# Where matmul operands begin in a partition: one start modulo 512 bytes for all of them

## The chip, the cores and the metric

One core of a Trainium2 chip runs the whole program: two blocks of a small language model over 256 tokens of width 1024. The metric is the device time of one execution in microseconds (us), the median of several runs.

## What is computed

The first block is a gated MLP mixer and a windowed attention; the second is a retention layer, an MLA attention and, behind each of these two, a PEER layer with 128 x 128 experts. Nearly all the work is projections of 256 tokens; of the two PEER layers, this is the core:

```python
q = (xb @ w_q).reshape(T, 8, 2, 128)
s = jnp.einsum('thcd,hckd->thck', q, sub_keys)          # scores of the sub-keys
# top 16 of each half, top 16 of their sums -> eidx, gate = softmax(top_s)
h = jax.nn.gelu(jnp.einsum('thkd,td->thk', u[eidx], xb))
return jnp.einsum('thk,thkd->td', gate * h, v[eidx])
```

The kernel computes it densely: `gelu(X u^T)` for all 16384 experts, times a table of gates that is zero outside the chosen ones, times `v`.

## The kernel before, in words

Activations lie transposed in SBUF: `xh` and `xl` are 128 partitions x 8 x 256 tokens. Every fp32 factor is held as two fp32r halves, a high and a low one. `mm3` (L146 to L150) multiplies two such pairs with three matmuls into one accumulator: high x high (L148), then L149, then L150.

- `unit` (L102) loads a block of 128 x 1024 weights over SP's DMA queue into a buffer `w` and splits it, 512 columns at a time, into `wh` (a cast on ScalarE, ACT, L139) and `wl` (a subtraction on VectorE, DVE, L140). Buffers are taken in turn from the pools that are open: `weights` has 3 `w` and 5 pairs `wh`/`wl` all the time; `w2` adds 3 and 5 in the first block and retention, each PEER layer adds 2 pairs, MLA 2 and 5.
- `o2` (L238): a slice of 128 weight columns is the stationary operand, 256 columns of `xh` or `xl` (in attention `xg`, in MLA the latents `cqT`, `ckT`) are the moving one: 24 matmuls a unit, 7872 on `xh`/`xl` in all. In PEER these are the `u` blocks.
- `out_unit` (L243): the stationary operand is a slice of 128 tokens of the activation (`wdh`/`wdl` in PEER, `yh`/`yl`, `oh`/`ol`), 512 columns of `wh`/`wl` move: 12 matmuls a unit. In PEER these are the `v` blocks.
- `o1_unit` (L229): the same with `xh`/`xl` as the stationary operand.

A tile scheduler sets order and waits from the code's order and priorities. A PEER layer runs thus: 16 `u` blocks with the query units between them; 48 `u` blocks, with the search for the best experts (`route`, DVE) woven in; 64 `u` blocks, with the gates of half the experts woven in (first pass: `gates`, L1143 and on, DVE and ACT, and small fp16 matmuls, L1169); 62 `v` blocks with the other half's gates (second pass); the 66 `v` blocks left.

Tiles stand in a partition one behind the other, in the order in which pools are opened and tiles asked for, each rounded up to 32 bytes. So small tiles push what stands behind them off any round address. The starts modulo 512 bytes, read from the built program:

| operand | before |
|---|---|
| `xh`, `xl` | 128 |
| `w`, `wh`, `wl` of `weights` | 160 |
| the same of every pool added later | 288 |
| `wdh`, `wdl`; MLA's `oh`, `ol` | 288 |
| `yh`, `yl` of the MLP mixer / of retention; `y0`, `y1` of attention | 32 / 96; 416 |
| `xg0`, `xg1` | 352 |
| `cqT`, `ckT` (two tiles each) | 288 |

A slice of a weight tile for `o2` begins a multiple of 512 bytes further, a 256-column slice of `xh` a multiple of 1024: they keep their tile's start modulo 512. Which buffer a matmul reads follows from the program's order.

Of the kernel before, what the change touches and what calls it, by code (L numbers as in the profile page):

```python
# [10 lines left out]
F32 = mybir.dt.float32  # L11
F32R = mybir.dt.float32r
# [9 lines left out]
KB = 8  # L22
# [10 lines left out]
U2 = 64  # L33
PASSES = ((0, 64, 64, 6), (64, 64, 62, 6))
NT = 8
GSCALE = 2.0 ** 15


class Net:
    def __init__(s, ctx, tc, aps):  # L40
        s.ctx, s.tc, s.nc, s.d = ctx, tc, tc.nc, aps
        nc = s.nc
        s.cp = ctx.enter_context(tc.tile_pool(name="consts", bufs=1))

        s.wbufs, s.pbufs, s.taken = [], [], [0, 0]
        s.more_weights(ctx, "weights", 3, NSPLIT)
        tc.cur_priority += 4 * AHEAD
        s.sp = ctx.enter_context(tc.tile_pool(name="small", bufs=4))
        s.ps = ctx.enter_context(tc.tile_pool(name="psum", bufs=4, space=bass.MemoryType.PSUM))
        s.xh = s.cp.tile([128, KB, 256], F32R, name="xh")  # L50
        s.xl = s.cp.tile([128, KB, 256], F32R, name="xl")
        s.iota = s.cp.tile([128, 128], F32, name="iota")
        nc.gpsimd.iota(s.iota, pattern=[[1, 128]], base=0, channel_multiplier=0,
                       allow_small_or_imprecise_dtypes=True)
        s.ident = s.cp.tile([128, 128], F32, name="ident")
        nc.gpsimd.memset(s.ident, 1.0)
        nc.gpsimd.affine_select(s.ident, s.ident, pattern=[[1, 128]], compare_op=ALU.is_equal, fill=0.0,
                                base=0, channel_multiplier=-1)
        s.eps = s.cp.tile([128, 1], F32, name="eps")
        nc.vector.memset(s.eps, EPS)  # L60
        with s.urgent():
            s.warm(s.eps)
        s.ident_r = s.cp.tile([128, 128], F32R, name="ident_r")
        nc.vector.tensor_copy(s.ident_r, s.ident)
# [81 lines left out]
    def mm3(s, out, a, b, start, stop):  # L146
# [2 lines left out]
        s.nc.tensor.matmul(out, a[0], b[1], start=False, stop=False)  # L149
        s.nc.tensor.matmul(out, a[1], b[0], start=False, stop=stop)  # L150

    def bcast(s, pool, ap, n, name, **kw):
        t = pool.tile([128, n], F32, name=name, **kw)
        s.nc.sync.dma_start(t, bass.AP(tensor=ap.tensor, offset=ap.offset, ap=[[0, 128], [1, n]]))
        return t

    def transposes(s, src, n):
# [160 lines left out]
    def gmlp(s, first, begin):  # L318
        nc, d = s.nc, s.d
        s.first = first  # L320
        s.h = first.tile([128, 2, D], F32, name="h")
        s.gains = first.tile([128, 2, KB], F32, name="gains")
        with ExitStack() as es:
            p = es.enter_context(s.tc.tile_pool(name="pa", bufs=1))
            with s.urgent():
# [18 lines left out]
            nc.sync.dma_start(s.gains, d["b_gains"].rearrange("p (a k) -> p a k", a=2))  # L344
            X = (s.xh, s.xl)
            v = p.tile([128, 2, 2048], F32, name="v")
            st = p.tile([128, 2, 4, 6], F32, name="vst")
            for c in range(4):
                outs = [s.mm(), s.mm()] if c else begun
                if c:  # L350
# [4 lines left out]
            lg = s.bcast(p, d["a_ln_g"], 2048, "lg")  # L355
# [83 lines left out]
    def swa(s, begun, begin):  # L439
        nc, d = s.nc, s.d  # L440
        with ExitStack() as es:
            p = es.enter_context(s.tc.tile_pool(name="pb", bufs=1))
# [3 lines left out]
            m = s.first.tile([128, D], F32, name="trash", tag="trash", bufs=1)[:, :384]  # L446
# [9 lines left out]
            kv = p.tile([128, 2, 256], F32, name="kv")  # L456
            kd = p.tile([128, 2, 2, 2, 64], F32, name="kd")
            sg = p.tile([128, 8, 256], F32, name="sg")
            xg = [p.tile([128, KB, 256], F32R, name=f"xg{i}") for i in range(2)]

            def gain_x():
                nc.vector.tensor_tensor(sg, s.xh.bitcast(F32), s.xl.bitcast(F32), op=ALU.add)
# [4 lines left out]
            fg = s.bcast(p, d["final_norm_g"], D, "fg")  # L467
            bkv = s.bcast(p, d["b_kv"], 256, "bkv")
            bq = s.bcast(p, d["b_bq"], D, "bq")
            sink = s.bcast(p, d["b_sinks"], 16, "sink")  # L470
            cs = p.tile([128, 2, 2, 32], F32, name="cs")
            nc.sync.dma_start(cs, d["swa_cs"].rearrange("p (a t f) -> p a t f", a=2, t=2))

# [179 lines left out]
    def retention(s, begun, begin):  # L653
        nc, d = s.nc, s.d
        with ExitStack() as es:
            p = es.enter_context(s.tc.tile_pool(name="pc", bufs=1))

            l = s.bcast(p, d["decay"], 8, "l")
            y, w, m, q0 = (p.tile([128, 8], F32, name=f"lg{i}") for i in range(4))
            nc.scalar.activation(y, l, AF.Exp)  # L660
            nc.vector.tensor_scalar(w, y, -1.0, 1.0, op0=ALU.mult, op1=ALU.add)
            nc.scalar.activation(q0, w, AF.Ln)
# [3 lines left out]
            nc.vector.reciprocal(w, w)  # L666
            nc.vector.tensor_tensor(q0, q0, w, op=ALU.mult)
            nc.vector.tensor_tensor(q0, q0, m, op=ALU.subtract)
            lgam = p.tile([128, 8], F32, name="lgam")
            nc.vector.scalar_tensor_tensor(lgam, q0, -1.0, y, op0=ALU.mult, op1=ALU.mult)  # L670
            nc.vector.tensor_scalar(m, m, -2.0, None, op0=ALU.mult)
            nc.vector.tensor_tensor(m, m, y, op=ALU.mult)
# [60 lines left out]
            def v_side(h):  # L733
                return [lambda f=f, tt=tt: f(h, tt) for f in (v_out, mix) for tt in range(2)]
# [3 lines left out]
            for c in range(8):  # L738
                tag = "acc" if c % 2 else "mm"
                outs[c] = [s.mm(tag), s.mm(tag)] if c else begun  # L740
                ap, c0 = (d["r_qk"], c * 4) if c < 4 else (d["r_v"], c * 4 - 16)
# [3 lines left out]
                s.weave([lambda u=u: s.o1_unit(s.unit(ap[c0 + u]), u, KB, X, outs[c]) for u in range(4)],  # L745
                        more[:2] + side[c - 1] + more[2:])
            late = v_side(3)
            gng = p.tile([128, 16], F32, name="gng")
            gnb = p.tile([128, 16], F32, name="gnb")
            nc.sync.dma_start(gng, d["gn_g"])  # L750
            nc.sync.dma_start(gnb, d["gn_b"])
            for t in (gng, gnb):
# [44 lines left out]
    def mla(s, begun, begin):  # L797
        nc, d = s.nc, s.d
        with ExitStack() as es:
            s.more_weights(es, "we", 2, NSPLIT)  # L800
            p = es.enter_context(s.tc.tile_pool(name="pe", bufs=1))
# [8 lines left out]
            cq = p.tile([128, 2, 384], F32, name="cq")  # L810
            ck = p.tile([128, 2, 256], F32, name="ck")
            kr = p.tile([128, 2, 2, 64], F32, name="kr")
            cqT = [p.tile([128, 3, 256], F32R, name=f"cqT{i}") for i in range(2)]
            ckT = [p.tile([128, 2, 256], F32R, name=f"ckT{i}") for i in range(2)]

            def latent(tt):
                for c, gain, a in ((cq, qg, acc[tt][0][:, :384]), (ck, kg, acc[tt][1][:, :256])):
# [11 lines left out]
            w = s.unit(d["m_uqr"][:, :1024]), s.unit(d["m_uqr"][:, 1024:])  # L829
# [28 lines left out]
            for u in range(2):  # L858
                w = s.unit(d["m_ukn"][u])
# [142 lines left out]
    def gate_tables(s, p, scratch, tabs):  # L1002
# [26 lines left out]
        rest = scratch[:, 0, :256]  # L1029
        nc.vector.tensor_scalar(rest, tp[:, :256], GSCALE, None, op0=ALU.mult)  # L1030
        nc.vector.tensor_copy(tabs[2][:, 0], rest)
# [15 lines left out]
    def peer(s, i, outs, begin):  # L1047
        nc, d = s.nc, s.d
        with ExitStack() as es:
# [53 lines left out]
            def gate(t0, b0, nb, act):  # L1103
                gp = s.gates(pg, t0, b0, nb, tabs, t0 // NT * act % 8 < act)
                hv = hst[:, b0:b0 + nb, t0:t0 + NT].rearrange("p b t -> p t b")
                nc.vector.scalar_tensor_tensor(hv, gp[:, :NT * nb].rearrange("p (t b) -> p t b", b=nb),  # L1106
                                               1.0 / (GSCALE * ALPHA), hv,
                                               op0=ALU.mult, op1=ALU.mult)
# [17 lines left out]
            for b0, nb, n, act in PASSES:  # L1126
                s.weave(blocks[:n], [lambda t=t: gate(t, b0, nb, act) for t in range(0, 256, NT)])
                blocks = blocks[n:]
# [14 lines left out]
    def gates(s, p, t0, b0, nb, tabs, act):  # L1143

        nc = s.nc
        i1t, i2t, gt = tabs
        sl = slice(t0, t0 + NT)
        a = p.tile([128, NT, 128], F16, name="ga", tag="ga", bufs=2)
        if act:
# [120 lines left out]
```

## Time and profile before

| | |
|---|---|
| median of 3 runs | 2291.69 us (2288.92 to 2292.26) |
| the profiled execution | 2291.83 us, its span 2290.1 us |
| TensorE (PE) busy | 2254.2 us, 98% |
| VectorE (DVE) busy | 1878.2 us, 82% |
| ScalarE (ACT) busy | 1532.3 us, 67% |
| granted clock of TensorE, mean | 0.997 |

The span is the time from the first to the last instruction; 1.7 us of the execution lie outside it. Ends of matmuls are modelled, since one begins before the last has drained: a matmul's row of 0.28 us does not mean 0.28 us of the engine. What it costs is the distance between two starts. PEld is the load of a stationary operand, which runs beside the matmul before.

### The profile page before, as it was taken

The numbers are of one execution on the slowest core, as the hardware profiler recorded it, in microseconds if no ns is written. First come the engines' busy times: TensorE is split into PE (matmuls) and PEld (weight loads), VectorE is DVE, ScalarE is ACT, GpSimd is POOL, SyncE is SP. The second block draws the span as 40 slices with busy tenths as digits, with TensorE's granted clock in tenths as the row PEclk, the third lists the DMA queues.
The fourth block names the chain that finished last, engine by engine and source line by source line (L and its number), as shares of the span: only waits on it lengthen the run. The fifth ranks groups of instructions, "written<-read, shape, count | busy, mean of one in ns | idle before, by whom it ended". The sixth has DMA issues, their size and how long they took to land. (4 is left out here: it accounts for less than half of the span.)

```text
span 2290.1 us, 43064 instructions
## 1 busy us (share of the span) xinstructions
PE 2254.2 (98%) x15726; PEld 2004.5 (88%) x15726; DVE 1878.2 (82%) x3685; ACT 1532.3 (67%) x3404; POOL 6.7 (0%) x15
## 2 busy tenths in 40 slices
PE   8999999999999999999999999999999999999998
PEld 6998877898999999977788878899999998777887
DVE  6867877567899899999986666689989999999666
ACT  5545865565555788888865546555569888887554
POOL 0000000000000000000000000000000000000000
PEclk9999999999999999999999999999999999999999
DMA  8655354354555555545455654355565554545564
GB/s 300 198 175 181 118 164 158 128 177 134 173 174 178 191 171 171 167 157 165 164 188 192 206 176 140 120 169 171 178 194 167 170 171 158 166 162 185 188 211 139
DMA packets 109224, 394.55 MB, mean 172 GB/s; under 512 B 12882, under 2 KB 13522, under 8 KB 108243
## 3 DMA queue, kind: packets, MB, share of 16 engines
q1 hardware_dynamic: 109010, 391.80, 52.4%
q8 instruction: 123, 2.02, 0.3%
q14 instruction: 91, 0.74, 0.1%
HBM read 390.70 MB, written 1.05 MB: 171 GB/s over the span
## 5 line engine op out<-in xcount | busy, mean ns | idle before, releaser
L139 ACT CAST wh<-w 128x512 fp32r<-128x512 f32 x1427 | 870.0, 614 | 556.6 <-PE mm L149 202.3
L140 DVE TENSOR_TENSOR wl<-w,wh 128x512 fp32r<-128x512 f32 x1427 | 970.7, 688 | 295.2 <-ACT wh L139 275.4
L148 PE MATMUL mm<-xh,wh 128*128 128x256 f32 x2624 | 745.9, 284 | 0.0
L149 PE MATMUL mm<-xl,wh 128*128 128x256 f32 x2624 | 739.0, 282 | 0.0
L150 PE MATMUL mm<-xh,wl 128*128 128x256 f32 x2624 | 738.2, 281 | 0.0
L148 PEld LDWEIGHTS mm<-xh,wh 128*128 128x128 f32 x2624 | 495.2, 189 | 1.7 <-issue 0.2
L149 PEld LDWEIGHTS mm<-xl,wh 128*128 128x128 f32 x2624 | 493.9, 188 | 1.7 <-issue 0.5
L150 PEld LDWEIGHTS mm<-xh,wl 128*128 128x128 f32 x2624 | 494.4, 188 | 0.4 <-DVE wl L140 0.4
L150 PE MATMUL acc<-wh,wdl 128*128 128x512 f32 x1024 | 404.2, 395 | 5.4 <-DVE wdl L140 5.2
L148 PE MATMUL acc<-wh,wdh 128*128 128x512 f32 x1024 | 408.5, 399 | 0.0
L149 PE MATMUL acc<-wl,wdh 128*128 128x512 f32 x1024 | 402.8, 393 | 0.0
L1155 ACT ACTIVATE gq<-iota,tab 128x128 bf16<-128x128 f32 x768 | 267.8, 394 | 5.6 <-DVE tab L1027 2.1
L150 PEld LDWEIGHTS acc<-wh,wdl 128*128 128x128 f32 x1024 | 192.3, 188 | 53.6 <-DVE wdl L140 8.9
L149 PEld LDWEIGHTS acc<-wl,wdh 128*128 128x128 f32 x1024 | 192.7, 188 | 42.2
L148 PEld LDWEIGHTS acc<-wh,wdh 128*128 128x128 f32 x1024 | 192.6, 188 | 41.0
L1106 DVE SCALAR_TENSOR_TENSOR hst<-mm,hst 128x512 f32<-128x512 f32 x128 | 172.7, 1349 | 0.0
L1164 DVE TENSOR_TENSOR gb<-ge,tabg 128x1024 f16<-128x1024 f16 x128 | 157.4, 1230 | 0.0
L139 ACT CAST wdh<-hst 128x256 fp32r<-128x256 f32 x256 | 102.7, 403 | 77.6 <-PE acc L149 69.2
L140 DVE TENSOR_TENSOR wdl<-hst,wdh 128x256 fp32r<-128x256 f32 x256 | 110.8, 433 | 31.0 <-ACT wdh L139 30.3
L1156 ACT ACTIVATE ga<-gq 128x512 f16<-128x512 bf16 x192 | 120.4, 627 | 2.7
L148 PE MATMUL mm<-wh,xh 128*128 128x512 f32 (+1 forms) x272 | 110.6, 406 | 0.3 <-ACT xh L139 0.2
L150 PE MATMUL mm<-wh,xl 128*128 128x512 f32 (+1 forms) x272 | 106.9, 394 | 0.5 <-DVE xl L140 0.3
(343 smaller groups left out, 2305.0 us busy)
## 6 DMA issues: line engine op xcount, KB each, us to landing
w<-in_p_u SPq DMA_DIRECT2D x256, 512.0 KB, 3.6
w<-in_p_v SPq DMA_DIRECT2D x256, 512.0 KB, 3.7
w<-in_p_q SPq DMA_DIRECT2D x32, 512.0 KB, 3.5
w<-in_a_v SPq DMA_DIRECT2D x16, 512.0 KB, 5.7
w<-in_a_g SPq DMA_DIRECT2D x16, 512.0 KB, 3.5
w<-in_a_u SPq DMA_DIRECT2D x16, 512.0 KB, 3.6
w<-in_a_out SPq DMA_DIRECT2D x16, 512.0 KB, 3.5
w<-in_r_qk SPq DMA_DIRECT2D x16, 512.0 KB, 3.5
```

Of the source, the lines that this page charges most:

```text
L139: s.nc.scalar.copy(hi, src)
L140: s.nc.vector.tensor_tensor(lo, src, hi.bitcast(F32), op=ALU.subtract)
L148: s.nc.tensor.matmul(out, a[0], b[0], start=start, stop=False)
L149: s.nc.tensor.matmul(out, a[0], b[1], start=False, stop=False)
L150: s.nc.tensor.matmul(out, a[1], b[0], start=False, stop=stop)
L1106: nc.vector.scalar_tensor_tensor(hv, gp[:, :NT * nb].rearrange("p (t b) -> p t b", b=nb), 1.0 / (GSCALE * ALPHA), hv, op0=ALU.mult, op1=AL ...
L1155: nc.scalar.activation(q[:, j, :], s.iota, AF.Square, scale=-1.0, bias=i2t[:, t:t + 1])
L1156: nc.scalar.activation(a[:, j0:j0 + 4, :], q, AF.Relu, scale=-1.0, bias=1.0)
L1164: nc.vector.tensor_tensor(b, e[:, None].to_broadcast([128, 2, NT, nb]), gt[:, :, sl, None].to_broadcast([128, 2, NT, nb]), op=ALU.mult)
```

## The change

No instruction is added, removed or moved: engine by engine the built programs have the same instructions in the same order with the same waits. What differs is where tiles stand. `xh` and `xl` get a pool of their own at the front, behind a pad of 56 words; small tiles (`sink`, `l`, `lgam`, `gng`, `gnb`, `vst`, `gains`) are put into rooms of whole 512 bytes; `apart` sets 48 words (192 bytes) ahead of `xg` and of the latents and fills up to 512 behind. Afterwards every fp32r operand of a matmul, moving or stationary, begins at 160 modulo 512, but for `xh`/`xl`, `xg`, `cqT` and `ckT`, which begin at 352 (160 + 192).

```diff
+LINE = 512
+EPS_ROOM = 48
+X_PAD = 56
+APART = 48
...
+        front = ctx.enter_context(tc.tile_pool(name="front", bufs=1))
+        front.tile([128, X_PAD], F32, name="pad")
+        s.xh = front.tile([128, KB, 256], F32R, name="xh")
+        s.xl = front.tile([128, KB, 256], F32R, name="xl")
+        s.sp = ctx.enter_context(tc.tile_pool(name="small", bufs=4))
         s.cp = ctx.enter_context(tc.tile_pool(name="consts", bufs=1))
+        s.eps = s.cp.tile([128, EPS_ROOM], F32, name="eps")[:, 0:1]
...
-        s.sp = ctx.enter_context(tc.tile_pool(name="small", bufs=4))
         s.ps = ctx.enter_context(tc.tile_pool(name="psum", bufs=4, space=bass.MemoryType.PSUM))
-        s.xh = s.cp.tile([128, KB, 256], F32R, name="xh")
-        s.xl = s.cp.tile([128, KB, 256], F32R, name="xl")
...
+    def lined(pool, n, name):
+        per = LINE // 4
+        return pool.tile([128, -(-n // per) * per], F32, name=name)[:, :n]
...
+    def apart(pool, shapes):
+        pool.tile([128, APART], F32, name="gap")
+        tiles = [pool.tile(shape, F32R, name=name) for shape, name in shapes]
+        return tiles, pool.tile([128, LINE // 4 - APART], F32, name="behind")
...
-        s.gains = first.tile([128, 2, KB], F32, name="gains")
+        s.gains = s.lined(first, 2 * KB, "gains").rearrange("p (a k) -> p a k", a=2)
...
-            xg = [p.tile([128, KB, 256], F32R, name=f"xg{i}") for i in range(2)]
+            xg, small = s.apart(p, [([128, KB, 256], f"xg{i}") for i in range(2)])
...
-            sink = s.bcast(p, d["b_sinks"], 16, "sink")
+            sink = small[:, :16]
+            s.spread(sink, d["b_sinks"])
...
+            small = s.lined(p, 80, "small")
+            l, y, w, m, q0, lgam = (small[:, 8 * i:8 * i + 8] for i in range(6))
+            gng, gnb = small[:, 48:64], small[:, 64:80]
...
-            cqT = [p.tile([128, 3, 256], F32R, name=f"cqT{i}") for i in range(2)]
-            ckT = [p.tile([128, 2, 256], F32R, name=f"ckT{i}") for i in range(2)]
+            turned, _ = s.apart(p, [([128, n, 256], f"{c}T{i}") for c, n in (("cq", 3), ("ck", 2)) for i in range(2)])
+            cqT, ckT = turned[:2], turned[2:]
```

## Rows read from the trace of the kernel before

**Rows 1.** The page: busy time, share of the span, instructions.
```profile
PE 2254.2 (98%) x15726; PEld 2004.5 (88%) x15726; DVE 1878.2 (82%) x3685; ACT 1532.3 (67%) x3404; POOL 6.7 (0%) x15
```
**Rows 2.** The longest of PE's waits: us in total, times, longest us.
```profile
PE acc L150 <- DVE wdl L140: 5.2, 6, 1.8
```
**Rows 3.** The page's groups: xcount | busy us, mean ns | idle before.
```profile
L148 PE MATMUL mm<-xh,wh 128*128 128x256 f32 x2624 | 745.9, 284 | 0.0
...
L150 PE MATMUL acc<-wh,wdl 128*128 128x512 f32 x1024 | 404.2, 395 | 5.4 <-DVE wdl L140 5.2
...
L148 PE MATMUL mm<-wh,xh 128*128 128x512 f32 (+1 forms) x272 | 110.6, 406 | 0.3 <-ACT xh L139 0.2
```
**Rows 4.** Timeline of PE, first and last of 60: `xh` 128, weights 160.
```profile
719.91 0.28 PE L148 MATMUL mm<-xh,wh 128*128 128x256 f32 x1
...
726.89 0.28 PE L150 MATMUL mm<-xh,wl 128*128 128x256 f32 x1
```
**Rows 5.** Timeline of PE, first and last of 24: `xh` 128, weights 288.
```profile
727.01 0.28 PE L148 MATMUL mm<-xh,wh 128*128 128x256 f32 x1
...
729.77 0.28 PE L150 MATMUL mm<-xh,wl 128*128 128x256 f32 x1
```
**Rows 6.** Timeline of PE, first and last of 43: `xg` 352, weights 160.
```profile
243.18 0.28 PE L148 MATMUL mm<-xg,wh 128*128 128x256 f32 x1
...
248.13 0.28 PE L148 MATMUL mm<-xg,wh 128*128 128x256 f32 x1
```
**Rows 7.** Timeline of PE: `xg` 352; the last is the 30th behind 252.57.
```profile
251.91 0.47 PE L149 MATMUL mm<-xg,wh 128*128 128x256 f32 x1
252.22 0.28 PE L150 MATMUL mm<-xg,wl 128*128 128x256 f32 x1
...
252.57 0.28 PE L150 MATMUL mm<-xg,wl 128*128 128x256 f32 x1
...
255.97 0.28 PE L150 MATMUL mm<-xg,wl 128*128 128x256 f32 x1
```
**Rows 8.** Timeline of PE, first and last of 30: weights 160 move, `wdh` 288.
```profile
1198.05 0.40 PE L148 MATMUL acc<-wh,wdh 128*128 128x512 f32 x1
...
1204.81 0.39 PE L150 MATMUL acc<-wh,wdl 128*128 128x512 f32 x1
```
**Rows 9.** Timeline of PE: weights 288 move, `wdh` 288; first, fourth and last of 12.
```profile
1205.04 0.39 PE L148 MATMUL acc<-wh,wdh 128*128 128x512 f32 x1
...
1205.74 0.39 PE L148 MATMUL acc<-wh,wdh 128*128 128x512 f32 x1
...
1207.55 0.39 PE L150 MATMUL acc<-wh,wdl 128*128 128x512 f32 x1
```
**Rows 10.** Timeline of PE, first and last of 30: weights 288, `xh` stationary, 128.
```profile
35.31 0.40 PE L148 MATMUL mm<-wh,xh 128*128 128x512 f32 x1
...
42.10 0.39 PE L150 MATMUL mm<-wh,xl 128*128 128x512 f32 x1
```
**Rows 11.** Windows: us, PE, PEld, DVE, ACT, POOL busy (x), PEclk, DMA share, GB/s.
```profile
551.00:640.00 89.00, 89.00 (x754) 88.86 (x753) 77.86 (x338) 48.52 (x106) 0.00 (x0) 1.00 0.53 172
640.00:740.00 100.00, 100.00 (x843) 99.83 (x842) 99.80 (x267) 51.48 (x105) 0.00 (x0) 1.00 0.54 175
740.00:771.00 31.00, 31.00 (x264) 31.00 (x263) 19.49 (x36) 17.42 (x37) 0.00 (x0) 1.00 0.69 220
771.00:960.00 189.00, 189.00 (x1930) 187.53 (x1929) 177.93 (x225) 167.40 (x420) 0.00 (x0) 1.00 0.52 168
960.00:1165.00 205.00, 202.27 (x1369) 162.83 (x1368) 202.01 (x293) 179.81 (x439) 0.00 (x0) 1.00 0.50 162
1165.00:1340.00 175.00, 175.00 (x771) 141.80 (x770) 116.98 (x195) 98.38 (x192) 0.00 (x0) 1.00 0.61 198
```
**Rows 12.** Waits from 771 to 960 us: us in total, times, longest us.
```profile
ACT wh L139 <- PE mm L149: 20.0, 26, 1.0
DVE wl L140 <- ACT wh L139: 11.1, 30, 0.4
```

More of the change, by code (lines that the diff above doesn't have):

```diff
@@ L58, in __init__ @@
                                 base=0, channel_multiplier=-1)
-        s.eps = s.cp.tile([128, 1], F32, name="eps")
         nc.vector.memset(s.eps, EPS)
@@ L150, in mm3, with spread @@
         s.nc.tensor.matmul(out, a[1], b[0], start=False, stop=stop)
+    @staticmethod
+    def lined(pool, n, name):
+        per = LINE // 4
+        return pool.tile([128, -(-n // per) * per], F32, name=name)[:, :n]
+    @staticmethod
+    def apart(pool, shapes):
+        pool.tile([128, APART], F32, name="gap")
+        tiles = [pool.tile(shape, F32R, name=name) for shape, name in shapes]
+        return tiles, pool.tile([128, LINE // 4 - APART], F32, name="behind")
+    def spread(s, t, ap):
+        s.nc.sync.dma_start(t, bass.AP(tensor=ap.tensor, offset=ap.offset, ap=[[0, 128], [1, t.shape[-1]]]))
     def bcast(s, pool, ap, n, name, **kw):
         t = pool.tile([128, n], F32, name=name, **kw)
-        s.nc.sync.dma_start(t, bass.AP(tensor=ap.tensor, offset=ap.offset, ap=[[0, 128], [1, n]]))
+        s.spread(t, ap)
         return t
@@ L346, in gmlp @@
             v = p.tile([128, 2, 2048], F32, name="v")
-            st = p.tile([128, 2, 4, 6], F32, name="vst")
+            st = s.lined(p, 48, "vst").rearrange("p (a c k) -> p a c k", a=2, c=4)
             for c in range(4):
@@ L656, in retention @@
             p = es.enter_context(s.tc.tile_pool(name="pc", bufs=1))
-            l = s.bcast(p, d["decay"], 8, "l")
-            y, w, m, q0 = (p.tile([128, 8], F32, name=f"lg{i}") for i in range(4))
+            small = s.lined(p, 80, "small")
+            l, y, w, m, q0, lgam = (small[:, 8 * i:8 * i + 8] for i in range(6))
+            gng, gnb = small[:, 48:64], small[:, 64:80]
+            s.spread(l, d["decay"])
             nc.scalar.activation(y, l, AF.Exp)
@@ L668, in retention @@
             nc.vector.tensor_tensor(q0, q0, m, op=ALU.subtract)
-            lgam = p.tile([128, 8], F32, name="lgam")
             nc.vector.scalar_tensor_tensor(lgam, q0, -1.0, y, op0=ALU.mult, op1=ALU.mult)
@@ L747, in retention @@
             late = v_side(3)
-            gng = p.tile([128, 16], F32, name="gng")
-            gnb = p.tile([128, 16], F32, name="gnb")
             nc.sync.dma_start(gng, d["gn_g"])
```

## The prediction

> **What bounds the kernel now.** I read the page first: TensorE is busy for 98% of the span [rows 1], and its longest wait adds up to 5.2 us [rows 2]. So the time is, to first order, the sum of the distances between the starts of matmuls, and the costliest group is the one of 128x256 matmuls on `xh` [rows 3]. Second the timeline of PE, since busy times of matmuls are modelled: there the reader is to take the first and the last start of a chain without a wait and divide by the number of steps. Third the windows, which show where another engine is full as well. They are cut at the stages of the first PEER layer [rows 11]; the second looks alike.
>
> The timeline holds the experiment already, because the kernel before mixes starts. With `xh` at 128 and weights at 160, 59 steps take 6.98 us: 118.3 ns each [rows 4]. With weights at 288, 23 steps take 2.76 us: 120.0 ns [rows 5]. Same instruction, same order, another buffer. For 512 columns the difference is larger: with the weights at 160 and `wdh` at 288 a step takes 6.76 / 29 = 233.1 ns [rows 8]; with both at 288 the chain of 12 falls, after three steps, to 1.81 / 8 = 226.3 ns [rows 9], 2.51 / 11 = 228.2 over all of it. So a matmul and the weight load beside it disturb each other, by an amount that their starts decide.
>
> **The pairing that the change makes** is 352 against 160 for 256 columns. `xg` in the first block has it today, and shows two rhythms: 4.95 / 42 = 117.9 ns [rows 6], and 3.40 / 30 = 113.3 ns [rows 7]. Each holds for as long as nothing interrupts it. The first chain ran on from one on weights at 288; the second began afresh on weights at 160, with its first steps at 0.31 and 0.12 us [rows 7]. After the change there are no weights at 288, and most chains begin afresh, behind gates or transposes, so I take 113.3 ns as the likelier; 117.9 is the other end.
>
> **The change, part by part.** Nothing is removed or added; ACT, DVE and DMA do the same work. DVE reads `w` and `wh` at equal starts in most of its splits today, so equal starts are nothing new to it, and I cost that at nothing. What is left are distances on PE.
>
> Before, 1788 of the 2624 matmuls of L148 read weights at 160 and 836 at 288 (counted in the program), as do those of L149 and L150: (1788 x 118.3 + 836 x 120.0) / 2624 = 118.8 ns. At 113.3 each saves 5.5 ns, where PE sets the pace. Stage by stage, for one PEER layer [rows 11]:
>
> - 28 blocks with the queries (before 640 us): DVE has 11 us of 89 free. 28 x 24 x 5.5 ns = 3.7 us.
> - 640 to 740: DVE is busy for 99.8 of 100 us. A faster PE only uses up its lead there; I count 0.
> - 740 to 771: DVE has 11.5 us free. Some 270 matmuls: 1.5 us.
> - First pass of gates, 64 blocks: 1536 x 5.5 ns = 8.4 us. DVE is the cover at risk: it idles 189.0 - 177.9 = 11.1 us there, all of it waiting for ACT, which waits for PE to free a buffer [rows 12]. So 8.4 fits, but barely, and DVE then starts the second pass with less lead.
> - Second pass: DVE is busy 202.0 of 205.0 us. `v` blocks gain nothing, and the lost lead comes due: I take -1.5 us, between 0 and -3.
> - 66 `v` blocks after it, PE alone: buffers come in turn, 5 at 160 and 2 at 288, so a step costs (5 x 233.1 + 2 x 228.2) / 7 = 231.7 ns now. With both operands at 160 they are as equal as in rows 9; I take 226.5. 792 x 5.2 ns = 4.1 us.
>
> That is 16.2 us a layer, 32.4 for two. Outside PEER: the gates of the MLP mixer (768 matmuls) and of retention (384) on `xh`: 1152 x 5.5 ns = 6.3 us. Their output products and those of attention and MLA (some 576 of 512 columns) become equal too: I price them as the `v` blocks, 2.9 us. The products with `xh` stationary (272 x 3 [rows 3], with MLA's some 900) go from starts 32 or 160 apart, at 234.1 ns for the latter [rows 10], to 320 apart. No row has that pairing. The bounds are 226.3 and 234.1, a gain of up to 7 us or nothing; I take nothing, because every unequal pairing above lies near 233. Attention's `xg` and MLA's latents are 192 and 120 matmuls: under 1 us either way, counted at 0.
>
> Sum: 32.4 + 6.3 + 2.9 = 41.6 us. The profiled execution took 2291.83 us, 0.1 above the median of the runs: **2250 us**.
>
> [...]
>
> **The rivals.**
>
> *The slow rhythm.* Chains on 352/160 settle at 117.9 ns. For it: it is what rows 6 show at this very pairing, for 42 steps. Against: rows 7. Then the 256-column steps that count, 2 x (672 + 270 + 1536) + 1152 = 6108, save 0.9 ns each, 5.5 us, and with the 512-column steps (8.2 + 2.9) the time is 2291.8 - 16.6 = 2275 us. If some stages settle fast and some slow, the time lies between the two.
>
> *Starts do not matter.* Then rows 4 and 5, or 8 and 9, would differ for another reason, such as the order of blocks, and the time would stay 2292 us. [...]
>
> *A third, slower rhythm: slower than before.* The place is the `o2` chain in the PEER layers. In the trace the pairing 352/160 occurs only on `xg`, whose chains begin behind attention's matmuls; in PEER they begin behind fp16 gates or fp32 scores. If they lock there into a step above today's, PE is slower in all 7872 matmuls, also where DVE is full now. The gain of 11.1 us at 512 columns pays for 1.4 ns; beyond 118.8 + 2.0 = 120.8 ns the kernel is slower by over 0.2%. Rows 5 show 120.0 for the worst pairing now, so this needs a step that no row has. At 122 ns it gives 2291.8 + 25.2 - 11.1 = 2306 us.
>
> **How the numbers follow.** A measurement of this kernel can tell about 0.2%, 4.6 us, from no change. The fast rhythm 0.51, 2250 us, itself uncertain by some 10 us: `xh` stationary could give 6 more, the lead lost to DVE 3 less or as much more, and chains that restart often cost before more than the means that I used. The slow rhythm, or a mixture: 0.36, 2256 to 2279. Starts do not matter: 0.08. Slower: 0.05. The range from 2238 to 2279 holds the first two cases but for their tails, some 8 in 10. Faster by over 0.2% are the first two, 0.87; within 0.2% 0.08; slower 0.05.
>
> **What would show it.** In the timeline of PE, a `u` chain of the first pass with steps of 113 or 118 ns tells the two rhythms apart; `v` chains behind the second pass at 226 to 227 ns, whatever buffer they use, show the equal starts at work. The window of the first pass should shrink from 189 towards 181 us with DVE near full, the one from 640 to 740 and the second pass hardly at all. ACT's and DVE's means at L139 and L140 should not move. The prediction is wrong if `v` chains still step at 233, if `u` chains step above 119, or if the second pass shrinks by more than 3 us: then DVE was not what bound it.

## The result, and the profile after

| | before | after |
|---|---|---|
| median (4 runs of each, one chip) | 2291.98 us (2288.92 to 2293.9) | 2257.42 us (2257.09 to 2258.18) |
| ratio, 95% interval | | 0.9851 (0.9834 to 0.9868): 1.5% faster |
| the profiled execution | 2291.83 us, span 2290.1 | 2258.18 us, span 2256.4 |

Forecast were 2250 us (2238 to 2279). The greater chance, 0.51, stood on the fast rhythm; what came is the case that had 0.36, a mixture of both rhythms: 34.6 us faster in place of 41.6.

The page of the kernel after, its busy line, answers to [rows 1]: PE's busy time falls by 42.8 us, DVE's and ACT's by 3 and 2. The span falls by 33.7 us only: PE idles 9.1 us more than before.

```profile
PE 2211.4 (98%) x15726; PEld 1972.0 (87%) x15726; DVE 1875.0 (83%) x3685; ACT 1530.3 (68%) x3404; POOL 6.2 (0%) x15
```

The longest of PE's waits (us in total, times, longest us), against [rows 2]: the wait for `wdl` has grown from 5.2 to 8.1 us.

```profile
PE acc L159 <- DVE wdl L149: 8.1, 11, 2.0
```

ACT's and DVE's splits of 512 columns, before and then after (xcount | busy us, mean ns | idle before): the means stay, so DVE and ACT, which read the same tiles, are not what the starts make faster.

```profile
L139 ACT CAST wh<-w 128x512 fp32r<-128x512 f32 x1403 | 858.5, 616 | 544.2 <-PE mm L149 202.3 <-PE acc L150 134.4 <-PE mm L150 67.4
L140 DVE TENSOR_TENSOR wl<-w,wh 128x512 fp32r<-128x512 f32 x1403 | 958.6, 691 | 291.7 <-ACT wh L139 272.0 <-ACT ss L1089 3.1 <-PE mm L149 2.2
...
L148 ACT CAST wh<-w 128x512 fp32r<-128x512 f32 x1403 | 858.9, 617 | 519.1 <-PE mm L158 153.0 <-PE acc L159 127.6 <-DMA w<-in_p_u 76.7
L149 DVE TENSOR_TENSOR wl<-w,wh 128x512 fp32r<-128x512 f32 x1403 | 952.3, 688 | 269.7 <-ACT wh L148 249.8 <-ACT ss L1115 3.2 <-PE mm L158 0.8
```

The windows of the first PEER layer, cut at the same instructions of PE as [rows 11] (us, PE, PEld, DVE, ACT, POOL busy (x), PEclk, DMA share, GB/s):

```profile
544.39:631.17 86.78, 86.78 (x753) 86.65 (x752) 77.40 (x335) 48.42 (x106) 0.00 (x0) 1.00 0.54 174
631.17:730.57 99.40, 97.76 (x844) 96.23 (x842) 99.19 (x268) 50.05 (x103) 0.00 (x0) 1.00 0.54 174
730.57:761.26 30.69, 30.69 (x263) 30.69 (x262) 20.72 (x39) 18.49 (x40) 0.00 (x0) 1.00 0.73 234
761.26:943.22 181.96, 181.93 (x1931) 180.65 (x1929) 174.45 (x223) 165.42 (x415) 0.00 (x0) 1.00 0.53 170
943.22:1151.10 207.88, 203.33 (x1370) 164.32 (x1368) 204.61 (x296) 181.47 (x444) 0.00 (x0) 0.98 0.51 164
1151.10:1322.41 171.31, 171.31 (x771) 141.75 (x769) 116.62 (x195) 98.63 (x192) 0.00 (x0) 1.00 0.65 202
```

Where PE sets the pace the windows shrink: the first pass from 189 to 181.96 us, the last `v` blocks from 175 to 171.31. The window full of DVE work (640 to 740 before) keeps its length, and the second pass, also full of DVE work, grows by 2.8 us between the same instructions.

The steps themselves, in the timeline of PE, kernel after: first and last start of a chain of the first pass (47 starts), of a gate chain of the MLP mixer (48; the line ahead of it is the output product behind which it runs on), and of two neighbours in the query stage (47 each).

```profile
771.93 0.28 PE L158 MATMUL mm<-xl,wh 128*128 128x256 f32 x1
...
777.15 0.28 PE L159 MATMUL mm<-xh,wl 128*128 128x256 f32 x1
...
77.89 0.39 PE L159 MATMUL acc<-wh,yl 128*128 128x512 f32 x1
78.12 0.28 PE L157 MATMUL mm<-xh,wh 128*128 128x256 f32 x1
...
83.66 0.28 PE L159 MATMUL mm<-xh,wl 128*128 128x256 f32 x1
...
550.96 0.28 PE L158 MATMUL mm<-xl,wh 128*128 128x256 f32 x1
...
556.19 0.28 PE L159 MATMUL mm<-xh,wl 128*128 128x256 f32 x1
556.86 0.28 PE L158 MATMUL mm<-xl,wh 128*128 128x256 f32 x1
...
562.28 0.28 PE L159 MATMUL mm<-xh,wl 128*128 128x256 f32 x1
```

5.22 / 46 = 113.5 ns in the first pass, where [rows 4] had 118.3; but 5.54 / 47 = 117.9 in the mixer; and in the query stage 5.23 / 46 = 113.7 beside 5.42 / 46 = 117.8. All of them have `xh`/`xl` at 352 and weights at 160. Both rhythms of [rows 6, 7] are there side by side: of 7497 starts on `xh`/`xl` that stand in chains of 20 or more, 5499 are in fast chains (below 115 ns), 1998 in slow ones (117.7 to 117.9). The 26 chains that run straight on behind an output product, as the one at 78.12 does, are all slow, here and in the run `shift` below.

Two 512-column chains of the kernel after, in the timeline of PE: `v` blocks behind the second pass (788 starts), and the first products with `xh`/`xl` stationary (183 starts).

```profile
1153.73 0.39 PE L158 MATMUL acc<-wl,wdh 128*128 128x512 f32 x1
...
1332.15 0.39 PE L159 MATMUL acc<-wh,wdl 128*128 128x512 f32 x1
...
15.23 0.39 PE L159 MATMUL mm<-wh,xl 128*128 128x512 f32 x1
...
56.90 0.39 PE L159 MATMUL mm<-wh,xl 128*128 128x512 f32 x1
```

178.42 / 787 = 226.7 ns over blocks from every buffer, against 233.1 in [rows 8]; and 41.67 / 182 = 229.0 ns for the pairing that no row had, against 234.1 in [rows 10].

### The profile page after: what moved, and what is told of

Same layout as the page of the kernel before. It is cut to its first block, busy times and chain, and to the rows that moved or that the text cites. A ratio compares the mean times of both kernels' runs of the same rounds, so it can differ in the third digit from the quotient of the medians.

```text
span 2256.4 us, 43064 instructions
## 1 busy us (share of the span) xinstructions
PE 2211.4 (98%) x15726; PEld 1972.0 (87%) x15726; DVE 1875.0 (83%) x3685; ACT 1530.3 (68%) x3404; POOL 6.2 (0%) x15
## 5 line engine op out<-in xcount | busy, mean ns | idle before, releaser
L157 PE MATMUL mm<-xh,wh 128*128 128x256 f32 x2624 | 737.5, 281 | 1.0 <-ACT hst L1095 1.0
L159 PE MATMUL mm<-xh,wl 128*128 128x256 f32 x2624 | 730.1, 278 | 2.4 <-DVE wl L149 1.9
L158 PE MATMUL mm<-xl,wh 128*128 128x256 f32 x2624 | 728.7, 278 | 0.0
```

What stands on the lines that cost most here:

```text
L157: s.nc.tensor.matmul(out, a[0], b[0], start=start, stop=False)
```

## The experiments

Theory: the start of the moving operand relative to that of the stationary one sets PE's step, and in stages where DVE is full a shorter step gains nothing. Rivals: another part of the change does it (the order of pools, the rooms of 512 bytes), or one start is good in itself.

**The two parts, each alone.** `x128` is the changed kernel with X back at 128: no pad, and 56 words more behind `eps`.

```diff
-EPS_ROOM = 48
-X_PAD = 56
+EPS_ROOM = 104
...
-        front.tile([128, X_PAD], F32, name="pad")
```

> The change with X put back to 128 modulo 512 as before; all other operands stay at 160. If the pairing of starts decides, every chain on xh steps at 118.3 ns as rows of before with weights at 160 do, the v blocks keep 226.7 ns, and products with xh stationary go back to 233: about 2275 us, 17 above the change. If only the equal starts of the weight buffers count and X's 192 bytes do nothing: 2257 us.

`x_only` is the kernel before with X alone moved to 352:

```diff
+        s.cp.tile([128, 56], F32, name="pad")
         s.xh = s.cp.tile([128, KB, 256], F32R, name="xh")
         s.xl = s.cp.tile([128, KB, 256], F32R, name="xl")
+        s.cp.tile([128, 72], F32, name="rest")
```

> The kernel before with nothing but X moved from 128 to 352: weights at 160 and 288, wdh at 288, as before. If the pairing of starts decides, chains on xh step at 113.4 or 117.8 ns on both kinds of buffers (as xg did before), the v blocks stay at 233 and 228: about 2269 us. If X's place is worth nothing without equal weight buffers: 2285 us or more.

Measured: `x128` 2278.48 us (2273.22 to 2280.39), ratio to before (2291.85 us beside it) 0.9932 (0.9916 to 0.9949); `x_only` 2269.05 us (2268.2 to 2271.86), 0.9903 (0.9886 to 0.9919). So X's place alone is worth 22.8 us and the rest of the change, the equal starts, 13.4; together 36.2, where the change gives 34.6. The timeline of PE in `x128`, first and last of 47 starts in the first pass: 5.45 / 46 = 118.5 ns, the step of before, though pools and rooms are those of the change.

```profile
779.47 0.28 PE L156 MATMUL mm<-xl,wh 128*128 128x256 f32 x1
...
784.92 0.27 PE L157 MATMUL mm<-xh,wl 128*128 128x256 f32 x1
```

In `x_only`, first a chain of 24 on weights at 288 (64 from X), then one of 48 on weights at 160 (192 from X):

```profile
770.98 0.28 PE L150 MATMUL mm<-xh,wh 128*128 128x256 f32 x1
...
773.58 0.28 PE L152 MATMUL mm<-xh,wl 128*128 128x256 f32 x1
...
113.57 0.28 PE L150 MATMUL mm<-xh,wh 128*128 128x256 f32 x1
...
119.11 0.28 PE L152 MATMUL mm<-xh,wl 128*128 128x256 f32 x1
```

2.60 / 23 = 113 ns and 5.54 / 47 = 117.9. Over all of `x_only`, of the starts in chains of 20 or more 3448 of 4682 at a distance of 192 are fast, and 1188 of 2009 at 64. So the pairing permits the fast rhythm and does not choose it.

**Why 192 further?** `x160` sets X to 160, equal to all the rest (`X_PAD = 8`, `EPS_ROOM = 96`).

> The change with X at 160 too, no 192 bytes. If for 256 columns equal starts are the wrong pairing (the latents at 288 on weights at 288 stepped at 117 to 120 ns before), chains on xh step at 119 to 120 ns and the time is about 2280 us, with the products on stationary xh at 226.7 in place of 229. If equal starts are best for every shape, chains on xh step at 113.4 ns throughout and the time is about 2250 us.

2283.53 us (2281.92 to 2290.05), ratio 0.9971 (0.9959 to 0.9982). The timeline of PE in `x160`: 183 starts with X stationary, then 47 of the first pass.

```profile
15.63 0.39 PE L159 MATMUL mm<-wh,xl 128*128 128x512 f32 x1
...
56.90 0.39 PE L159 MATMUL mm<-wh,xl 128*128 128x512 f32 x1
...
779.84 0.28 PE L158 MATMUL mm<-xl,wh 128*128 128x256 f32 x1
...
785.35 0.28 PE L159 MATMUL mm<-xh,wl 128*128 128x256 f32 x1
```

41.27 / 182 = 226.8 ns: for 512 columns no distance in any run is better than equal starts. 5.51 / 46 = 119.8: for 256 columns they are worse than a distance of 480 (before). The two lengths want different distances, and that is what the 192 bytes are for.

**Other distances**, one run of each (X at 256, 320, 384 and 416 by `X_PAD` 32, 48, 64, 72, and `EPS_ROOM` less by the same; before took 2292.29 us on this chip):

> X at 256 modulo 512, 96 bytes past the weights at 160. The pairing theory says that the pair has a step of its own, in every chain on xh and in all stages, whichever it is: 113.4 (floor), 117.8, or 118 to 120 ns. It doesn't say which; between 64 and 192, which both show 113.4 and 117.8, it may be either. A step that differs by stage but not by what stands ahead of the chain would speak against it.

> X at 320, 160 bytes past the weights. As for 256; if 192 is one point of a stretch of good distances, 113.4 ns shows here too, and more often than at 192 if its middle lies below 192: at best 2245 us, with every chain at 113.4. If 192 is a single good point: 118 to 120 ns and about 2280 us.

> X at 384, 224 bytes past the weights. As for 320, on the other side of 192: 113.4 ns in more chains if the stretch's middle lies above 192, 118 to 120 ns and about 2280 us if 192 is a single good point.

> X at 416, 256 bytes past the weights, the farthest from equal starts. If distance alone counted, this were the best: 113.4 ns throughout, 2245 us. The pairing theory has no such order: for 512 columns 256 apart stepped at 230.8 in the kernel before, neither best nor worst; I expect 117 to 120 ns, 2270 to 2283 us.

X at 256 has one step in every stage, 119.5 to 120.0 ns, as the theory says. X at 320 never shows 113.4, so 192 is not one point of a stretch that reaches to 160; it has two rhythms too, 117.3 and 118.7 to 118.9. X at 384, 118.0 to 118.7, is as forecast if 192 has no good neighbour on that side either. X at 416 steps as expected for 256 columns; for 512 the 230.8 was no guide, since the first products with X stationary (186 starts) step at 41.96 / 185 = 226.8 ns there, as with equal starts:

```profile
15.10 0.40 PE L159 MATMUL mm<-wh,xl 128*128 128x512 f32 x1
...
57.06 0.39 PE L159 MATMUL mm<-wh,xl 128*128 128x512 f32 x1
```

**A distance of 64, and everything 128 bytes further.** `x224` has `X_PAD = 24`, `EPS_ROOM = 80`; `shift` keeps the distance of 192 and moves all of it:

```diff
-        front.tile([128, X_PAD], F32, name="pad")
+        front.tile([128, 32 + X_PAD], F32, name="pad")
```

> The changed kernel with X at 224 in place of 352 (pad 24 words, room behind eps 80): the distance from the weights is 64 in place of 192; attention's and MLA's operands keep 192. Theory (64 is as good as 192: with X alone moved, chains on weights at 288, a distance of 64, showed both 113.4 and 117.8 ns): the time of the change within some 4 us, 2253 to 2262 us, the same two rhythms. Rival (64 falls mostly into the slow rhythm): all chains at 117.8 ns, the first passes lose 2 x 1536 x 4.2 ns = 12.9 us and other fast stages some more, 2270 us or above. The products with X as the stationary operand, 448 apart, have no row so far: 229 to 234 ns.

> The changed kernel with 32 words more in the pad at the front: every fp32r operand begins 128 bytes further, weights at 288 and X and the latents at 480 modulo 512, the distance of 192 kept. Theory (the distance between the moving and the stationary operand decides): the chains of 256 columns at 113.4 or 117.8 ns, those of 512 at 226.7, and the time of the change, 2257 us within some 4 us. Rival (the starts themselves decide, 160 is special): steps of other lengths, 118 to 120 and 230 or more, and a time between 2270 and 2292 us.

`shift` took 2258.55 us (2257.61 to 2265.54), ratio 0.987 (0.9853 to 0.9887), the time of the change; in the timeline of PE its chain of the first pass steps 5.22 / 46 = 113.5 ns:

```profile
773.66 0.28 PE L158 MATMUL mm<-xl,wh 128*128 128x256 f32 x1
...
778.88 0.28 PE L159 MATMUL mm<-xh,wl 128*128 128x256 f32 x1
```

So, as far as a move of all by 128 bytes can tell, it is the distance, not the start. `x224` took 2274.62 us (2272.48 to 2275.62), ratio 0.9928 (0.9911 to 0.9944): its rival was right. Of its 7665 starts in chains on `xh`/`xl` none is in a fast one. The same chain of the first pass in its timeline, 5.42 / 46 = 117.8 ns:

```profile
776.15 0.28 PE L158 MATMUL mm<-xl,wh 128*128 128x256 f32 x1
...
781.57 0.28 PE L159 MATMUL mm<-xh,wl 128*128 128x256 f32 x1
```

All the distances in one table (X's start minus the weights', modulo 512; X is the moving operand for 256 columns and the stationary one for 512, where moving minus stationary is the negative of it; ns per step from chains of 20 and more starts, for 512 columns from the first and longest, and the time of the kernel where X stands at that distance):

| distance of X from weights | kernel | 256 columns, X moves | 512 columns, X stationary | us |
|---|---|---|---|---|
| 0 | `x160` | 119.3 to 120.0 | 226.8 | 2283.53 |
| 64 | `x224` | 117.8 | 233.3 | 2274.62 |
| 96 | `x256` | 119.5 to 120.0 | 234.2 | 2289.82 |
| 160 | `x320` | 117.3 or 118.7 to 118.9 | 233.4 | 2277.38 |
| 192 | after, `shift` | 113.4 or 117.8 | 229.0 | 2257.42, 2258.55 |
| 224 | `x384` | 118.0 to 118.7 | 233.3 | 2282.5 |
| 256 | `x416` | 119.3 to 120.0 | 226.8 | 2282.95 |
| 480 | `x128` | 118.0 to 118.5 | 233.3 | 2278.48 |

No other of these places of X comes near the change. And the table repeats after 256 bytes: 0 and 256 have the same steps for both lengths, 224 and 480 too, and the chains on weights at 288 of the kernel before, a distance of 352, step at 119.5 to 120.2 ns as those at 96. On these pairs the start modulo 256 tells all that the start modulo 512 does; 192 against 448 was not run for 256 columns in a kernel of its own.

**What stands ahead of a chain.** If a chain takes its rhythm from how it begins, other work ahead of it should flip it. `entry` is the changed kernel with the small products of the mixer ahead of its gate chains in place of the output products, and retention's transposes ahead of its gates. In the mixer:

```diff
-                mix(f, ugs.pop(f))
                 if 0 < f < 14:
                     out(f - 1)
+                mix(f, ugs.pop(f))
```

(retention's transposes move ahead of its gate in the same way)

> The change with two steps reordered: the MLP mixer's small mixing matmuls, and retention's two transposes, come right ahead of the gate's chain on xh, where an output product of 512 columns stood. If what stands ahead of a chain sets which of the two rhythms it falls into, the gates of the MLP mixer and of retention step at 113.5 ns in place of 117.8: about 1100 x 4.3 ns = 4.7 us less, 2253 us. If the rhythm belongs to the stage or the buffers, they stay at 117.8 ns and the time at 2257 us.

2256.68 us (2255.27 to 2261.18), ratio 0.9848 (0.9832 to 0.9865): no difference from the change that can be told. But the 13 gate chains of the mixer that ran straight on behind an output product, and were slow, now begin behind the small products and are fast; over their twelve periods that saves 2.1 us. The mixer's first three gates flipped too, but they do so in `shift` as well, where nothing is reordered. One of the 13 in the timeline of PE, 47 starts, 5.21 / 46 = 113.3 ns:

```profile
106.71 0.28 PE L158 MATMUL mm<-xl,wh 128*128 128x256 f32 x1
...
111.92 0.28 PE L159 MATMUL mm<-xh,wl 128*128 128x256 f32 x1
```

Retention's gates stayed slow in 12 of 16. So what runs ahead plays a part, but not by its kind alone: in `x_only`, where the output products' own operands stand at other distances, 7 of 11 chains at 192 behind one are fast, and in the query stage of the change, chains behind the same small fp32 matmuls (L1113) are fast and slow in turn.

**Does DVE bound the second pass?** `relief_before` and `relief_after` halve one of DVE's instructions there, and only there:

```diff
-        nc.vector.tensor_tensor(b, e[:, None].to_broadcast([128, 2, NT, nb]),
-                                gt[:, :, sl, None].to_broadcast([128, 2, NT, nb]), op=ALU.mult)
+        nc.vector.tensor_tensor(b[:, :half], e[:, None].to_broadcast([128, half, NT, nb]),
+                                gt[:, :half, sl, None].to_broadcast([128, half, NT, nb]), op=ALU.mult)
```

(`half` is 1 in the second pass and 2 in the first; the matmul reads `b[:, k % half, j, :]`)

> The kernel before, with DVE relieved in the second pass of gates alone: of the two halves of the gate table (high, low) only the high one is multiplied out there, and the small fp16 matmuls read it twice. It leaves out the low half of the gates of experts 64 to 127 of each row. PE, ACT and the DMA queue keep the same instructions in the same order; on DVE 32 instructions of about 1.24 us a layer become half as long, about 19 us a layer. Theory (DVE bounds the second pass, which is why a faster PE gains nothing there): the pass falls to what PE needs, 744 steps of about 231.7 ns and some 14 us of gates' matmuls, 187 us in place of about 203, so about 2292 - 2 x 16 = 2260 us. Rival (PE bounds the pass and DVE only looks full): no change, 2292 us.

> The same edit in the changed kernel; it leaves out the same low half. Theory (DVE bounds the second pass): PE needs 744 x 226.7 ns and 14 us, 183 us in place of 201, so about 2257 - 2 x 18 = 2221 us, and the distance to the kernel before with the same relief grows from 34.5 us to some 40 to 48 us, since now the v blocks of this pass pay out too and the lead that the first pass takes from DVE no longer comes due. Rival (PE bounds the pass): no change, 2257 us, and the distance stays 34.5 us.

Beside 2290.19 us for the kernel before, `relief_before` took 2283.05 us (2280.58 to 2284.82), ratio 0.9965 (0.9953 to 0.9978), and `relief_after` 2246.12 us (2241.91 to 2249.53), ratio 0.9802 (0.9786 to 0.9818). The rival, no change, falls; but the gains are 7.1 and, against the change's 2257.42, 11.3 us in place of 32 and 36, and the distance between the two, 36.9 us, has grown by no more than it is uncertain. The windows from 1000 to 1140 us, inside the second pass, tell why: of the kernel after,

```profile
1000.00:1140.00 140.00, 136.68 (x899) 108.61 (x898) 140.00 (x205) 122.20 (x298) 0.00 (x0) 0.99 0.50 163
```

and of `relief_after`:

```profile
1000.00:1140.00 140.00, 140.00 (x939) 113.03 (x938) 136.74 (x215) 128.81 (x315) 0.00 (x0) 1.00 0.55 174
```

DVE was full and PE was not; relieved, PE is full and DVE no longer quite, and PE gets through 939 matmuls in place of 899. So DVE does bound the pass, but PE idles only 2% of it: my estimate of what PE needs there was too low. Between the same instructions of PE, the two reliefs take 3.8 and 6.3 us off the first layer's second pass, and the one after loses to the one before only 0.6 us from 967 us (by the clock of before) to 1165, where the change without relief loses 3.1. But the change has two stretches at the lower clock there (lines in the next section) and `relief_after` one, at 1.7 us each: so 1.7 of the 2.5 us between 3.8 and 6.3 is clock, and the loss of 3.1 is not shown to be DVE's doing.

## Why the prediction was right, and where it missed

The mechanism (starts set PE's step, DVE covers part of the gain), the direction and the range were right; the rhythm taken as likelier was not the one that came throughout. Set beside the terms of the sum, by the starts of the same instructions of PE in both profiles (gain in us, both PEER layers together, the first layer cut as in [rows 11]):

| term | predicted | measured |
|---|---|---|
| query stage | 7.4 | 4.2 |
| DVE's search (640 to 740) | 0 | 1.5 |
| 740 to 771 | 3.0 | 1.6 |
| first passes | 16.8 | 13.4 |
| second passes | -3.0 | -2.6 |
| `v` blocks behind them | 8.2 | 7.3 |
| all outside PEER | 9.2 | 8.4 |
| sum, before rounding | 41.6 | 33.7 |

- **The step that failed** is "most chains begin afresh, behind gates or transposes, so I take 113.3 ns". Neither half of it holds. The gates of the mixer and of retention mostly do not begin afresh: 26 of the 32 run straight on behind an output product, in chains that are all slow. In the query stage the chains do begin afresh, and every second one is slow all the same. The first passes are fast throughout. The row behind the 113.3 was also weaker than it was read: of the 31 starts from 252.57 on in [rows 7], 21 read weights at 288 (counted in the program), a distance of 64; only the first ten have the pairing of the change. That this pairing does hold the fast rhythm for long is therefore partly luck.
- **The first passes** lost 3.4 us of their term although every chain there is fast. The mean step, restarts left out, goes from 118.7 to 113.7 ns: 5.0 ns, not 5.5, since a chain takes three slower steps before it settles (122, 116 and 114 ns, medians of the first layer's 30 chains there; 113.3 from then on). The rest is matmuls that the schedule runs outside these windows, and in the second layer a wait of 0.73 us for DVE's `gb` (timeline of PE, 1683.94 us). DVE as the cover held in the first layer: it still idles 7.5 of the 182 us, and PE stands still for 0.03 us.
- **Outside PEER** the sum came out near by errors of opposite sign, which is luck. The gates, 1152 matmuls, step at 117.5 ns in place of 119.3: 2.0 us in all and not 6.3. The products with X stationary, priced at nothing because every unequal pairing in the rows lay near 233, took 229.0 ns in place of 233.2 to 234.1: about 900 times 4.2 to 5.1 ns, some 4 us.
- **`v` blocks**: 226.7 ns in the long chain behind the second pass, as forecast (226.5). So none of the three signs of being wrong came: `v` chains left 233, no `u` chain steps above 119, and the second pass did not shrink.
- **DVE as the cover**: next to nothing was gained where it is full. That the second passes gave back 2.6 us where I took 3.0 is luck: the first layer's lost 2.8 us, where the clock alone took 3.4 (lines below), and the second layer's, where the clock stayed up, lost nothing. In `shift`, with the same distances, the two together lose 0.6. How the reliefs bear on it stands above.
- **The slow rhythm** was priced at 2275 us; `x224`, where every chain falls into it, took 2274.62 (with X stationary as slow as before).
- **Starts do not matter** is dead: `x128` and `x224` have the instructions and the order of the change and lose some 21 and 17 us, and in the table above the step of 512 columns goes from 226.8 to 234.2 ns by the place of one operand. That a matmul and the weight load beside it disturb each other was my reading of such steps; the runs show the steps, not what passes between the two. No chain in any run here settled below 113 ns for 256 columns and 226 for 512.

How a wait of PE for DVE turns into time, where the first pass of the kernel after goes over into `v` blocks: the timeline of PE (start, us, what it is, and in brackets the idle time before it with its releaser), then windows of this place and of a second one.

```profile
955.96 0.28 PE L309 MATMUL acc<-ident_r,xl 128*128 128x128 f32 x1
957.19 0.50 PE L157 MATMUL acc<-wh,wdh 128*128 128x512 f32 x1 [0.95 <-ACT wdh L148]
957.52 0.40 PE L158 MATMUL acc<-wl,wdh 128*128 128x512 f32 x1
958.20 0.80 PE L159 MATMUL acc<-wh,wdl 128*128 128x512 f32 x1 [0.28 <-DVE wdl L149]
958.79 0.63 PE L157 MATMUL acc<-wh,wdh 128*128 128x512 f32 x1
959.22 0.63 PE L158 MATMUL acc<-wl,wdh 128*128 128x512 f32 x1
```

```profile
955.00:960.00 5.00, 3.77 (x16) 2.81 (x16) 5.00 (x7) 1.09 (x4) 0.00 (x0) 0.80 0.34 111
960.00:965.00 5.00, 5.00 (x25) 3.84 (x24) 3.02 (x6) 2.36 (x5) 0.00 (x0) 0.85 0.31 105
...
1098.00:1100.00 2.00, 2.00 (x7) 1.51 (x6) 2.00 (x4) 1.29 (x3) 0.00 (x0) 0.50 0.67 229
1100.00:1102.00 2.00, 2.00 (x21) 1.38 (x20) 2.00 (x5) 1.99 (x6) 0.00 (x0) 0.65 0.08 31
```

A faster PE gets there before the first `wdh` and `wdl` are split, waits 1.23 us, and then runs for a while at a lower granted clock: six steps from 958.79 us on take 2.56 us, 427 ns each, and the mean granted clock of the first two windows is 0.80 and 0.85, which costs (0.20 + 0.15) x 5 = 1.75 us more than the wait. At about 1095 us the same happens once more behind a wait of 2.03 us, with a granted clock of 0.50 and 0.65 in the last two, for (0.50 + 0.35) x 2 = 1.7 us. In the kernel before, the granted clock of this pass was 1.00 [rows 11].

But such a stretch does not follow every such wait. The same instruction waits 1.76 us in the kernel before, and 2.04 us in the second layer of the kernel after, and both times the clock stays at 1.00. First the two waits, before and after, then their windows:

```profile
1111.27 0.50 PE L150 MATMUL acc<-wh,wdl 128*128 128x512 f32 x1 [1.76 <-DVE wdl L140]
...
2013.45 0.50 PE L159 MATMUL acc<-wh,wdl 128*128 128x512 f32 x1 [2.04 <-DVE wdl L149]
...
1110.00:1115.00 5.00, 3.73 (x30) 2.96 (x31) 5.00 (x8) 3.91 (x11) 0.00 (x0) 1.00 0.61 210
...
2010.00:2015.00 5.00, 2.96 (x14) 2.11 (x13) 5.00 (x8) 4.01 (x12) 0.00 (x0) 1.00 0.46 134
```

So in this layer the lost lead itself costs one new wait of 1.23 us and 0.27 us more of an old one; the 3.4 us of clock came with it in this execution and need not in another. What decides whether the clock falls behind such a wait stays open here.

## What to carry to other kernels

Where PE is at 98% and steps of one instruction differ from buffer to buffer, compare the operands' starts modulo 512 bytes (modulo 256 gave the same on every pair that was run here): with fp32r a few hundred bytes of padding were worth 1.5%. Try the distance between moving and stationary operand for each length of the moving one, and read the steps of long chains, not the busy times. Before counting the gain stage by stage, look for the engine next in line: where it was full here, a shorter step paid next to nothing (1.5 us in DVE's search, -2.6 in the second passes) and cost a wait of 1.23 us.

## What was not expected of the hardware

- A chain of 256 columns at a distance of 192 has two steady steps, 113.4 and 117.8 ns, and nothing between; `shift` has the same chains fast and slow as the change, but for a few. A distance of 160 has two as well, 117.3 and 118.7. That it hangs on what ran ahead is shown by `entry` for 13 chains; what in it decides stays open.
- A distance of 64 held 113 ns in `x_only`, where chains at 192 stood between, and in [rows 7] behind ten starts at 192, and was never fast in `x224`. That it can carry the fast rhythm on but does not enter it by itself would fit, and was not tried.
- For 512 columns equal starts, and starts 256 bytes apart, were the fastest of the distances run (226.8 ns); for 256 columns they were among the slowest (119.3 to 120.0 ns).
- Behind waits of 1.23 and 2.03 us in the midst of full work PE ran a stretch at a lower granted clock (down to 0.50) that cost another 1.7 us each; waits of 1.76 and 2.04 us for `wdl` went by at 1.00.
